# Square Fourier tiles with a tile for the odd column, and rings that begin at one offset

## The chip, the cores and the metric

The kernel runs on one core of a Trainium2 chip, as one program. The metric is the device time of one execution in microseconds (us). The kernel before takes 1317.71 us, the median of three runs from 1316.97 to 1318.9.

## The reference

The input is 256 tokens of 1024 features (float32) and a memory of 256 tokens. Four layers follow, with the mixers Fourier, grouped-query attention, dilated attention, Fourier; each has four heads of attention to the memory beside its mixer, a gate, an output projection, a residual and a layer norm. Two layers of another kind come after them. The change touches the Fourier mixer, which is

```
def fourier_mix(h):
    hg = h.reshape(B, S, 4, D // 4)                 # 4 groups of 256 features
    y = jnp.fft.fftn(hg, axes=(1, 3), norm="ortho").real   # over tokens, and over a group's features
    return y.reshape(B, S, D)

s = jnp.einsum("bshd,bmhd->bhsm", qm, mk) * d**-0.5   # memory attention, 4 heads of 64
o = jnp.einsum("bhsm,bmhd->bshd", softmax(s), mv)
y = (concat([mixer, o]) * silu(gate)) @ w_out         # the branch, 1024 + 256 wide
x = layer_norm(8 ** 0.25 * x + y)
```

and, by the place of some tiles alone, the two layers behind (low-rank attention, a state-space scan, a gated spatial part and a wide MLP).

## The kernel before, in words

**Products.** Every float32 product is made of three TensorE matmuls: each operand is split into a high and a low half (ScalarE copies the high half, VectorE subtracts for the low one), and `Group.add` (L221) issues high by high, high by low, low by high. The 256x1024 activations stand transposed in `xT`, as halves. Weights stream from HBM on SyncE's DMA queue into a ring `raw`; ScalarE (L162) and VectorE (L164) split them into rings `wh` and `wl`.

**Order.** The program is written for a framework that schedules the instructions of each engine from a model of their costs; the order on an engine is that of its schedule, and every engine runs its own in order. Tiles of a ring are given out in turn.

**The rings of operands.** `ph` (20 slots, L399) holds halves of activations in the first four layers, `ph2` (12 slots, L964) in the two layers behind. As the built program places them, the tiles `xT`, `raw`, `wh` and `wl` begin 192 bytes above a multiple of 512. A slot of `ph` takes 2080 bytes, so its slots begin at all sixteen multiples of 32 modulo 512, and those of `ph2` begin at 96. In the products that project to the model's width (512 columns), a tile of `ph` or `ph2` is the stationary operand and `wh` or `wl` the moving one. Such products with `ph2` are 768 in the MLP and 192 in the output projections of the last two layers; those of `ph` are some 480 in the output projections of the first four.

**A Fourier layer** (`layer_fourier`, layers 0 and 3). For each of four groups two PSUM tiles of 258 columns are made, one for each half of the tokens: 129 cosine columns (0 to 128) and 129 sine columns of the transform over features. `split` (L671; ScalarE and VectorE lines L193 and L194) brings each into `uh` and `ul`. The column 128 of the cosines, the odd one, is copied by GpSimd (L673) into `mid`, where it stands in column 32g for group g; the rest of `mid` is zero. `positions(g)` makes the transform over tokens for the 128 regular cosine and sine columns (256-column matmuls into `sc`), adds and subtracts the two parts on VectorE, and moves 127 rows by a DMA on GpSimd's queue (L693) into `sg[0:127, 2g+1]`. `middle()` does the same for the odd columns of all groups: six matmuls into `sc`, a ScalarE copy (L701), and a DMA on GpSimd's queue (L702) that brings four rows into row 127 of `sg`'s blocks 1, 3, 5 and 7. So no block with an odd number is complete before the transfer of L702 has landed.

**What comes behind.** The gates' projections (256-column matmuls `acc<-xT,w`) are turned into `th` by ScalarE (L512; the ring has two tiles), and VectorE combines gate and branch (L513, L515). A combined block c is split by ScalarE and GpSimd (`finish_y`, L545 and L201) and is then the stationary operand of the output projection (`mm_out`), that is `acc<-wh,ph`, `acc<-wl,ph` and `tp<-wh,ph` with 512 columns. L515 makes two blocks at a time, so it always needs a block with an odd number. The memory attention is woven in as `pair_dense`: scores, softmax, transposes of the probabilities (L534, `tp<-ident,pt`), a split into `PTh` and `PTl`, and the products `pv` with the memory's values (`mv_99` and `mv_100` are the high and low halves).

Of the kernel before, what the change touches and what calls it, by code (L numbers as in the profile page):

```python
# [9 lines left out]
F32 = mybir.dt.float32  # L10
# [7 lines left out]
P = 128  # L18
# [58 lines left out]
def kernel(ctx: ExitStack, tc: tile.TileContext, x_in, wall, vec, tabs, small, out, dbg=None):  # L77
    nc = tc.nc
    V, A, G, PE = nc.vector, nc.scalar, nc.gpsimd, nc.tensor
# [11 lines left out]
    def scp(shape):  # L91
        return psum.tile(shape, F32, tag="sc", name="sc", bufs=2)

    def tpp(shape):
        return psum.tile(shape, F32, tag="tp", name="tp", bufs=2)
# [7 lines left out]
    def pt(shape, dt=F32):  # L103
        return ab.tile(shape, dt, tag="P", name="pt", bufs=4)
# [76 lines left out]
    def W(key, i, ahead=AHEAD):  # L181
        n = where[(key, i)]
        while state["split"] <= min(n + ahead, len(order) - 1):
            while state["raw"] <= min(state["split"] + 1, len(order) - 1):
                load_raw(state["raw"])
                state["raw"] += 1
            split_w(state["split"])
            state["split"] += 1
        return wts[n]

    def split(h, l, src, scale=None, eng=None):
        if scale is None:
            A.copy(out=h, in_=src)  # L193
            return (eng or V).tensor_tensor(out=l, in0=src, in1=h.bitcast(F32), op=ALU.subtract).ins  # L194
        else:
            A.activation(out=h, in_=src, func=AF.Copy, scale=scale)
            return (eng or V).scalar_tensor_tensor(
                out=l, in0=src, scalar=scale, in1=h.bitcast(F32), op0=ALU.mult, op1=ALU.subtract).ins
# [49 lines left out]
    def hl(pair, f):  # L248
        return f(pair[0]), f(pair[1])
# [3 lines left out]
    def run(steps):  # L253

        while True:
            try:
                next(steps)
            except StopIteration as e:
                return e.value
# [139 lines left out]
    def ph(shape, dt=F32R):  # L399
        return pool1.tile(shape, dt, tag="ph", name="ph", bufs=20)  # L400
# [48 lines left out]
    for i in range(4):  # L449
# [3 lines left out]
        for c in range(2):  # L453
            for kk in range(2):
                k = 2 * i + kk
# [142 lines left out]
    def tail(key, blk0, by_class=False):  # L598

        half = lambda hf: slice(hf, T, 2) if by_class else slice(hf * P, (hf + 1) * P)  # L600
        ps = yield from proj_N(key, blk0, True, lambda t, k, hf: t[:, k, half(hf)])
        qm = (ph([P, 2, T]), ph([P, 2, T]))
        for hf in range(2):
            t = pool1.tile([P, 512], F32, tag="tq", name="tq", bufs=2)
            th = pool1.tile([P, 256], F32, tag="tqh", name="tqh", bufs=2)
            with tc.high_priority():
                A.activation(out=t[:, 0:256], in_=ps[hf][:, 0:256], func=AF.Copy, scale=0.125)
                A.activation(out=th, in_=ps[hf][:, 256:512], func=AF.Tanh, scale=0.5)
                V.scalar_tensor_tensor(out=t[:, 256:512], in0=th, scalar=1.0, in1=ps[hf][:, 256:512], op0=ALU.add, op1=ALU.mult)
            tp = tpp([P, 4, P])  # L610
            for j in range(4):
                PE.transpose(tp[:, j, :], t[:, j * P:(j + 1) * P], ident)
            split(qm[0][:, :, half(hf)], qm[1][:, :, half(hf)], tp[:, 0:2, :])
            A.copy(out=sg[:, 8:10, half(hf)], in_=tp[:, 2:4, :])
        has_gate.update((8, 9))
        return qm

    def gates(key, blk):
        for b in range(2):
            ps = yield from proj_T(key, blk + b)  # L620
            for j in range(2):
                gate(ps[j], 4 * b + 2 * j)

    def out_and_norm(i, order_, next_order=None):
        gb = []

        def add(hf, blk, ps):
            c = slice(blk * 512, (blk + 1) * 512)
            with tc.high_priority():
                V.scalar_tensor_tensor(out=x[:, hf, c], in0=x[:, hf, c], scalar=ALPHA, in1=ps, op0=ALU.mult, op1=ALU.add)  # L630
                stats(hf, blk)
                if blk == 1:
                    layer_norm(hf, gb, next_order)

        def ready(n):
            if order_[n] not in has_y:
                return False
            if n == 5 and not gb:
                gb.extend(load_gb(i + 1))
                if next_order == "rms":  # L640
                    gn[0] = load_gn(10496)
            for c in order_[n:n + 3]:
                if c in has_y and c not in ys:
                    finish_y(c)
            return True

        ys.clear()
        yield from mm_out(add, f"o{i}", lambda n: (ys[order_[n]][:, 0, :], ys[order_[n]][:, 1, :]), 10, i == 2, ready, i)
        for t in (has_gate, has_branch, has_y):
            t.clear()  # L650
        dump(f"h{i + 1}", x)

    def layer_fourier(i):
        j = i // 3
        key = f"a{j}"
        dc = W(f"dftc{j}", 0)
        dt_ = [W(f"dftt{j}", n) for n in range(2)]
        uv = []

        mid = ph([P, 2, 2, P])  # L660
        G.memset(mid.bitcast(F32), 0.0)
        for g in range(4):
            uh, ul = ph([P, 2, 258]), ph([P, 2, 258])
            for hf in range(2):
                tp = tpp([P, 258])
                gr = Group(tp, 2)
                for kc in range(2):
                    k = 2 * g + kc
                    gr.add((xTh[:, k, hf * P:(hf + 1) * P], xTl[:, k, hf * P:(hf + 1) * P]),
                           hl(dc, lambda t: t[:, kc * 258:(kc + 1) * 258]))  # L670
                split(uh[:, hf, :], ul[:, hf, :], tp)  # L671
            for n, t in enumerate((uh, ul)):
                G.tensor_copy(out=mid[:, n, :, 32 * g:32 * g + 1], in_=t[:, :, 128:129])  # L673
            uv.append((uh, ul))
        qm = run(tail(key, 0))


        odd = [pool1.tile([P, 2, T], F32, tag="odd", name="odd", bufs=2) for _ in range(2)]

        def positions(g):  # L680
            sp = scp([P, 2, T])
            bk = {}
            for part in range(2):
                gr = Group(sp[:, part, :], 2, bk)
                for kc in range(2):
                    gr.add(hl(uv[g], lambda t: t[:, kc, 129 * part:129 * part + P]),
                           hl(dt_[kc], lambda t: t[:, part * T:(part + 1) * T]))
            r = pt([P, T])
            A.copy(out=r, in_=sp[:, 1, :])
            V.tensor_tensor(out=sg[:, 2 * g, :], in0=sp[:, 0, :], in1=r, op=ALU.add)  # L690
            o = odd[g // 2][:, g % 2, :]
            sc_read.append(V.tensor_tensor(out=o, in0=sp[:, 0, :], in1=r, op=ALU.subtract).ins)
            G.dma_start(sg[0:127, 2 * g + 1, :], o[1:128])  # L693

        def middle():
            sp = scp([P, T])
            gr = Group(sp, 2)
            for kc in range(2):
                gr.add(hl((mid[:, 0], mid[:, 1]), lambda t: t[:, kc, :]), hl(dt_[kc], lambda t: t[:, 0:T]))
            r = pt([P, T])  # L700
            sc_read.append(A.copy(out=r, in_=sp).ins)  # L701
            G.dma_start(sg[127:128, 1:8:2, :], r[0:128:32, :])  # L702
            has_branch.update(range(8))

        def fill():
            for g in range(4):
                positions(g)
                yield
            middle()
            yield from gates(key, 1)  # L710
            yield from out_and_norm(i, ORDER[0], "rms" if i == DEPTH - 1 else None)

        weave(fill(), [(lambda: True, lambda m=m: memory_pair(qm, m)) for m in range(2)], 2, 2)
# [145 lines left out]
    def layer_dilated(i):  # L859
# [84 lines left out]
        for hf in range(2):  # L944
            nc.gpsimd.dma_start(x[:, hf, :], scratch[hf * P:(hf + 1) * P, :])

    layer_fourier(0)
    nc.scalar.dma_start(rtab, tabs[:, 0:512].rearrange("p (h k d) -> p h k d", h=2, k=4))
    for hf in range(2):
        t = pt([P, 512])  # L950
# [11 lines left out]
    p2 = ctx.enter_context(tc.tile_pool(name="p2", bufs=1))  # L962

    def ph2(shape, dt=F32R):  # L964
        return p2.tile(shape, dt, tag="ph2", name="ph2", bufs=12)
# [68 lines left out]
    def layer2(l):  # L1034
# [15 lines left out]
        rn = p2.tile([P, 2, 2], F32, tag="rn", name="rn")  # L1050
        kr = p2.tile([P, 2, 1, 32], F32, tag="kr", name="kr")
        dtr = p2.tile([P, 2, 6], F32, tag="dtr", name="dtr")
        cqT = [ph2([P, 2, T]) for _ in range(3)]
        ckvT = [ph2([P, 2, T]) for _ in range(2)]

# [375 lines left out]
        gr = {}  # L1431
# [34 lines left out]
    for hf in range(2):  # L1466
        t = [ph2([P, 512], F32) for _ in range(2)]
# [174 lines left out]
```

## Time and profile before

| what | value |
|---|---|
| median of three runs | 1317.71 us (1316.97 to 1318.9) |
| the profiled execution | 1315.77 us |
| its span | 1314.1 us |
| granted TensorE clock, mean | 0.994 |
| TensorE busy | 1260.3 us, 96% |
| VectorE busy | 979.2 us, 75% |
| ScalarE busy | 751.4 us, 57% |
| GpSimd busy | 187.1 us, 14% |

The span runs from the first to the last instruction; 1.7 us of the execution lie around it. Busy shares are of the span. TensorE's matmuls overlap in their pipeline, so the time from the start of one to the start of the next, its pitch, is what a matmul costs in a dense row, and it is shorter than its printed duration.

### The profile page before, as it was taken

What the parts mean: (1) busy time and instruction counts of PE and PEld (TensorE: products, weight loads), DVE (VectorE), ACT (ScalarE), POOL (GpSimd) and SP (SyncE); (2) the same over time, 40 slices, a digit from 0 to 9 for tenths busy, and PEclk for the clock granted to TensorE, in tenths of its full rate; (3) what the DMA queues carried; (4) which work ended last, traced back from release to release, by engine and by line L of the source; (5) the groups of instructions that cost most, each with busy time, mean ns of one, the idle gap of its engine ahead of it and who ended that gap; (6) DMA issues with size and microseconds to landing.
All of it is one profiled execution on the core that took longest, in us unless ns stands there. A gap on an engine that the chain in (4) does not pass through costs nothing. (4 is left out here: it accounts for less than half of the span.)

```text
span 1314.1 us, 20879 instructions
## 1 busy us (share of the span) xinstructions
PE 1260.3 (96%) x7102; PEld 1063.0 (81%) x7102; DVE 979.2 (75%) x1994; ACT 751.4 (57%) x1689; POOL 187.1 (14%) x290
## 2 busy tenths in 40 slices
PE   7999998899999999998998999999999999999997
PEld 6987796578778778897986897788887897788886
DVE  7788887788777877886777896676666887675654
ACT  5664576655555555663653784565554775565543
POOL 1131500111211211222132201000001201000000
PEclk9999999999999999999998999999999999999999
DMA  8574542354435444455564643476665454476661
GB/s 287 174 216 144 170 153 65 112 177 140 126 120 162 140 148 129 128 176 166 185 194 130 198 137 112 129 243 189 188 186 162 134 153 140 131 223 183 189 191 49
DMA packets 64059, 209.48 MB, mean 159 GB/s; under 512 B 8520, under 2 KB 10192, under 8 KB 63952
## 3 DMA queue, kind: packets, MB, share of 16 engines
q1 hardware_dynamic: 60480, 203.33, 50.6%
q0 software_dynamic: 1888, 3.15, 0.8%
q10 hardware_dynamic: 1584, 1.67, 0.4%
q8 instruction: 56, 0.92, 0.3%
q14 instruction: 51, 0.42, 0.1%
HBM read 204.97 MB, written 2.10 MB: 158 GB/s over the span
## 5 line engine op out<-in xcount | busy, mean ns | idle before, releaser
L164 DVE TENSOR_TENSOR wl<-raw,wh 128x512 fp32r<-128x512 f32 (+3 forms) x756 | 504.8, 695 | 181.0 <-ACT wh L162 167.3
L162 ACT CAST wh<-raw 128x512 fp32r<-128x512 f32 (+3 forms) x756 | 440.9, 607 | 305.4 <-PE acc L221 93.0
L221 PE MATMUL acc<-wh,xT 128*128 128x512 f32 (+3 forms) x1120 | 350.8, 388 | 5.8 <-DVE xT L194 2.5
L221 PEld LDWEIGHTS acc<-wh,xT 128*128 128x128 f32 x1120 | 206.8, 189 | 45.9 <-DVE xT L194 5.1
L221 PE MATMUL acc<-wh,ph 128*128 128x512 f32 (+2 forms) x672 | 225.1, 390 | 6.7 <-ACT ph L545 2.3
L221 PE MATMUL acc<-wl,xT 128*128 128x512 f32 (+3 forms) x560 | 214.6, 384 | 0.2 <-DVE wl L164 0.2
L221 PEld LDWEIGHTS acc<-wh,ph 128*128 128x128 f32 x672 | 125.2, 189 | 38.1 <-ACT ph L193 4.6
L221 PE MATMUL acc<-wl,ph 128*128 128x512 f32 (+2 forms) x336 | 130.4, 388 | 0.0
L221 PE MATMUL acc<-xT,wh 128*128 128x256 f32 x672 | 127.9, 286 | 0.0
L221 PEld LDWEIGHTS acc<-wl,xT 128*128 128x128 f32 x560 | 106.1, 190 | 17.6 <-DVE wl L164 0.5
L221 PEld LDWEIGHTS acc<-xT,wh 128*128 128x128 f32 x672 | 105.9, 191 | 1.4
L221 PE MATMUL sc<-wh,ph 128*128 128x512 f32 (+1 forms) x328 | 104.5, 369 | 0.1
L204 POOL TENSOR_TENSOR rot<-rot,t 128x256 f32<-128x256 f32 (+3 forms) x84 | 61.4, 752 | 253.2 <-DVE t L724 172.2
L221 PE MATMUL acc<-xT,wl 128*128 128x256 f32 x336 | 95.6, 285 | 0.0
L1417 PE MATMUL tp<-xT,wh 128*128 128x512 f32 x224 | 80.9, 395 | 0.0
L221 PEld LDWEIGHTS acc<-wl,ph 128*128 128x128 f32 x336 | 63.8, 190 | 11.5
L221 PEld LDWEIGHTS sc<-wh,ph 128*128 128x128 f32 x328 | 59.8, 188 | 12.2 <-ACT ph L193 0.5
L221 PEld LDWEIGHTS acc<-xT,wl 128*128 128x128 f32 x336 | 64.1, 191 | 0.5
L1418 PE MATMUL tp<-xT,wl 128*128 128x256 f32 x224 | 62.8, 281 | 0.0
L221 PE MATMUL sc<-wl,ph 128*128 128x512 f32 (+1 forms) x164 | 60.9, 371 | 0.0
L365 POOL TENSOR_SCALAR st<-st 128x1 f32<-128x1 f32 x10 | 3.1, 306 | 386.7 <-ACT pt L360 386.7
L201 POOL TENSOR_TENSOR ph<-sg,ph 128x256 fp32r<-128x256 f32 x40 | 36.5, 937 | 128.2 <-ACT ph L545 128.1
(268 smaller groups left out, 2017.6 us busy)
## 6 DMA issues: line engine op xcount, KB each, us to landing
raw<-in_wall_dram SPq DMA_DIRECT2D x338, 512.0 KB, 4.3
raw<-in_wall_dram SPq DMA_DIRECT2D x20, 384.0 KB, 3.6
ph<-in_vec_dram SPq DMA_DIRECT2D x20, 256.0 KB, 5.8
raw<-in_wall_dram SPq DMA_DIRECT2D x8, 422.0 KB, 3.9
gn<-in_vec_dram SPq DMA_DIRECT2D x5, 512.0 KB, 4.8
raw<-in_wall_dram SPq DMA_DIRECT2D x6, 288.0 KB, 3.3
raw<-in_wall_dram SPq DMA_DIRECT2D x6, 256.0 KB, 3.5
x<-in_x_in_dram SPq DMA_DIRECT2D x2, 512.0 KB, 8.2
```

The costliest lines, as they stand in the source:

```text
L162: ih = A.copy(out=h[:, :k], in_=t[:, c]).ins
L164: il = V.tensor_tensor(out=l[:, :k], in0=t[:, c], in1=h[:, :k].bitcast(F32), op=ALU.subtract).ins
L201: G.tensor_tensor(out=out, in0=a, in1=b, op=ALU.subtract)
L204: G.tensor_tensor(out=out, in0=a, in1=b, op=ALU.add)
L221: done[0] = PE.matmul(out=self.out, lhsT=s, rhs=m, start=(i == 1), stop=(i == bk["n"]), skip_group_check=True).ins
L365: G.tensor_scalar(out=v, in0=ssx[hf][:, 0:1], scalar1=ssx[hf][:, 1:2], scalar2=RMS_EPS, op0=ALU.add, op1=ALU.add)
L1417: PE.matmul(out=ps[c], lhsT=h_, rhs=xT[:, k, :, :], start=(k == 0), stop=False, skip_group_check=True)
L1418: done[0] = PE.matmul(out=ps[c][:, 0, :], lhsT=l_, rhs=xTh[:, k, :], start=False, stop=(k == 7), skip_group_check=True).ins
```

## The change

`uh` and `ul` hold two tiles of 128 columns a half, 2048 bytes for each partition and no longer 2064. `split` takes columns 0 to 127 and 129 to 256 of the PSUM tile; column 128 is split from PSUM straight into `mid`, by ScalarE and VectorE (one 128x1 instruction each for every half and group: 8 and 8 a layer), and GpSimd's copies (8 a layer) are gone. The stationary operand in `positions` is indexed accordingly. In the two last layers a tile of 224 bytes that nobody uses stands ahead of the ring `ph2`.

```
         for g in range(4):
-            uh, ul = ph([P, 2, 258]), ph([P, 2, 258])
+            uh, ul = ph([P, 2, 2, P]), ph([P, 2, 2, P])
...
-                split(uh[:, hf, :], ul[:, hf, :], tp)
-            for n, t in enumerate((uh, ul)):
-                G.tensor_copy(out=mid[:, n, :, 32 * g:32 * g + 1], in_=t[:, :, 128:129])
+                split(uh[:, hf], ul[:, hf], tp.rearrange("p (a k) -> p a k", a=2)[:, :, 0:P])
+                split(mid[:, 0, hf, 32 * g:32 * g + 1], mid[:, 1, hf, 32 * g:32 * g + 1], tp[:, 128:129])
...
-                    gr.add(hl(uv[g], lambda t: t[:, kc, 129 * part:129 * part + P]),
+                    gr.add(hl(uv[g], lambda t: t[:, kc, part, :]),
...
         dtr = p2.tile([P, 2, 6], F32, tag="dtr", name="dtr")
+        p2.tile([P, 56], F32, tag="pad", name="pad")
         cqT = [ph2([P, 2, T]) for _ in range(3)]
```

Modulo 512 bytes, the tiles of the built programs begin at:

| tiles | before | after |
|---|---|---|
| `xT`, `raw`, `wh`, `wl` | 192 | 192 |
| `ph`, 20 slots | all multiples of 32 | 320 |
| `ph2`, 12 slots | 96 | 320 |
| `PTh`, `PTl`, `th`, `mkT`, `mv` | 320 | 320 |

The two last layers have the same instructions in the same order on every engine. In the first four the schedule differs at three places: in layer 0, at one small place of layer 2 (the dilated attention), and in layer 3. Two of them follow.

TensorE in layer 0, kernel before, from the last matmuls of `middle` (`sc<-wh,ph` and `sc<-wl,ph`): gates (`acc<-xT`) and transposes (`tp<-ident,pt`) alternate.

```order
L221 MATMUL sc<-wl,ph 128x256
L221 MATMUL sc<-wh,ph 128x256
L221 MATMUL acc<-xT,wl 128x256
L221 MATMUL acc<-xT,wh 128x256 x2
L534 MATMUL tp<-ident,pt 128x128 x2
L221 MATMUL acc<-xT,wl 128x256
L534 MATMUL tp<-ident,pt 128x128 x2
```

This pattern of gates goes on, with the other four transposes in it, and the stretch ends with

```order
L221 MATMUL acc<-xT,wl 128x256
L221 MATMUL pv<-PTh,mv_99 128x512
L221 MATMUL pv<-PTl,mv_99 128x512
L221 MATMUL pv<-PTh,mv_100 128x512
L221 MATMUL pv<-PTh,mv_99 128x512
L221 MATMUL pv<-PTl,mv_99 128x512
L221 MATMUL pv<-PTh,mv_100 128x512
L221 MATMUL acc<-wh,ph 128x512
```

In all 37 gate matmuls stand between `middle` and the first matmul of the output projection (`acc<-wh,ph`). The same place in the changed kernel:

```order
L221 MATMUL sc<-wl,ph 128x256
L221 MATMUL sc<-wh,ph 128x256
L534 MATMUL tp<-ident,pt 128x128 x8
L221 MATMUL pv<-PTh,mv_99 128x512
L221 MATMUL pv<-PTl,mv_99 128x512
L221 MATMUL pv<-PTh,mv_100 128x512
L221 MATMUL pv<-PTh,mv_99 128x512
L221 MATMUL pv<-PTl,mv_99 128x512
L221 MATMUL pv<-PTh,mv_100 128x512
L221 MATMUL acc<-wh,ph 128x512
```

All gates now stand ahead of `middle`'s six matmuls; behind them are 8 transposes and 6 products `pv`.

TensorE in layer 3, changed kernel, from `middle`'s last matmul to the output projection:

```order
L221 MATMUL sc<-wh,ph 128x256
L221 MATMUL acc<-xT,wh 128x256
L221 MATMUL acc<-xT,wl 128x256
L221 MATMUL acc<-xT,wh 128x256 x2
L221 MATMUL acc<-xT,wl 128x256
L221 MATMUL acc<-xT,wh 128x256
L534 MATMUL tp<-ident,pt 128x128 x2
L221 MATMUL acc<-xT,wh 128x256
L534 MATMUL tp<-ident,pt 128x128 x2
L221 MATMUL acc<-xT,wl 128x256
L534 MATMUL tp<-ident,pt 128x128 x4
```

Before, 36 gate matmuls stand in that place, with the transposes among them, and one product `pv` ahead of the output projection's first two; now there are 8 gate matmuls, and four products `pv` follow.

VectorE at the same place of layer 3, before and then after (PTl is the low half of the transposed probabilities, which `pv` needs; `sg` is the branch, whose odd blocks wait for the transfer of L702):

```order
L164 TENSOR_TENSOR wl<-raw,wh 128x512 x4
L515 SCALAR_TENSOR_TENSOR sg<-sg,th 128x512 x2
L194 TENSOR_TENSOR PTl<-tp,PTh 128x512 x2
L513 SCALAR_TENSOR_TENSOR th<-th,acc 128x512
L164 TENSOR_TENSOR wl<-raw,wh 128x512
```

```order
L164 TENSOR_TENSOR wl<-raw,wh 128x512 x4
L515 SCALAR_TENSOR_TENSOR sg<-sg,th 128x512
L194 TENSOR_TENSOR PTl<-tp,PTh 128x512
L515 SCALAR_TENSOR_TENSOR sg<-sg,th 128x512
L194 TENSOR_TENSOR PTl<-tp,PTh 128x512
L513 SCALAR_TENSOR_TENSOR th<-th,acc 128x512 x2
```

One L194 now stands between the two L515; in both kernels the first L515 is ahead of it.

## Rows read from the trace of the kernel before

**Rows 1.** Part 1 of the page: busy time of each engine.

```profile
PE 1260.3 (96%) x7102; PEld 1063.0 (81%) x7102; DVE 979.2 (75%) x1994; ACT 751.4 (57%) x1689; POOL 187.1 (14%) x290
```

**Rows 2.** Windows, layer 0: PE, PEld, DVE, ACT, POOL busy; clock, DMA, GB/s.

```profile
25.00:85.00 60.00, 58.19 (x419) 52.72 (x418) 46.36 (x94) 39.39 (x92) 8.12 (x16) 1.00 0.64 203
```

**Rows 3.** PE timeline, output projection: start, duration, instruction, [idle <-releaser].

```profile
94.16 0.39 PE L221 MATMUL acc<-wh,ph 128*128 128x512 f32 x1
...
96.89 0.40 PE L221 MATMUL acc<-wh,ph 128*128 128x512 f32 x1
...
99.69 0.39 PE L221 MATMUL acc<-wh,ph 128*128 128x512 f32 x1
```

**Rows 4.** Chain that ended last, MLP of the last layer: start, length, step.

```profile
1296.03 5.60 PE acc L221 x24
```

**Rows 5.** ScalarE splits by form: busy and mean ns; idle and releasers.

```profile
L193 ACT CAST ph<-acc 128x128 fp32r<-128x128 f32 x48 | 11.3, 277 | 4.8 <-DVE ph L194 3.4 <-DVE t L724 1.3
```

**Rows 6.** PE timeline, layer 0, from the end of `middle` to the output projection.

```profile
74.75 0.28 PE L221 MATMUL acc<-xT,wl 128*128 128x256 f32 x1
...
76.03 0.40 PE L221 MATMUL acc<-xT,wh 128*128 128x256 f32 x2
...
77.83 0.40 PE L221 MATMUL acc<-xT,wh 128*128 128x256 f32 x2
78.07 0.60 PE L534 MATMUL tp<-ident,pt 128*128 128x128 f32 x4
78.42 0.36 PE L221 MATMUL acc<-xT,wl 128*128 128x256 f32 x1
...
81.99 0.50 PE L221 MATMUL pv<-PTl,mv 128*128 128x512 f32 x1 [0.84 <-DVE PTl L194]
...
82.56 0.39 PE L221 MATMUL acc<-wh,ph 128*128 128x512 f32 x1
```

**Rows 7.** ScalarE timeline, layer 0.

```profile
75.16 0.37 ACT L701 COPY pt<-sc 128x256 f32<-128x256 f32 x1
...
81.50 0.59 ACT L512 ACTIVATE th<-acc 128x512 f32<-128x512 f32 x1
81.99 0.70 ACT L545 CAST ph<-sg 128x256 fp32r<-128x256 f32 x2
```

**Rows 8.** GpSimd timeline, layer 0.

```profile
75.81 0.61 POOL L702 DMA_DIRECT2D sg<-pt  x1 [9.36 <-ACT pt L701]
```

**Rows 9.** VectorE timeline, layer 0.

```profile
80.04 1.30 DVE L515 SCALAR_TENSOR_TENSOR sg<-sg,th 128x512 f32<-128x512 f32 x2
```

**Rows 10.** Line L702: its transfers, one in layer 0, one in layer 3.

```profile
DMA to landing us min/median/max: 3.0/3.6/4.1
```

**Rows 11.** Line L693: its eight transfers.

```profile
DMA to landing us min/median/max: 2.1/2.5/3.9
```

**Rows 12.** PE timeline, layer 3, the same place.

```profile
663.53 0.40 PE L221 MATMUL acc<-xT,wh 128*128 128x256 f32 x2
...
669.40 0.51 PE L221 MATMUL acc<-wh,ph 128*128 128x512 f32 x1 [0.29 <-ACT ph L545]
```

**Rows 13.** GpSimd timeline, layer 3.

```profile
664.61 0.61 POOL L702 DMA_DIRECT2D sg<-pt  x1 [9.15 <-ACT pt L701]
```

**Rows 14.** VectorE timeline, layer 3.

```profile
667.67 1.30 DVE L515 SCALAR_TENSOR_TENSOR sg<-sg,th 128x512 f32<-128x512 f32 x2 [0.55 <-DMA sg<-pt]
668.88 1.28 DVE L194 TENSOR_TENSOR PTl<-tp,PTh 128x512 fp32r<-128x512 f32 x2
```

**Rows 15.** PE timeline, layer 2, scores and transposes of the dilated attention.

```profile
378.92 0.66 PE L534 MATMUL tp<-ident,pt 128*128 128x128 f32 x4
...
383.00 0.44 PE L534 MATMUL tp<-ident,pt 128*128 128x128 f32 x2 [0.69 <-DVE pt L836]
```

**Rows 16.** Windows, columns as in rows 2: three stretches with long waits of TensorE.

```profile
612.00:622.00 10.00, 6.90 (x32) 5.78 (x32) 8.29 (x15) 1.93 (x4) 4.83 (x8) 0.83 0.57 175
698.00:712.00 14.00, 8.35 (x31) 6.56 (x29) 8.48 (x15) 4.96 (x13) 3.42 (x6) 0.76 0.08 28
786.00:797.00 11.00, 9.04 (x40) 6.46 (x41) 8.50 (x23) 4.96 (x15) 2.92 (x3) 0.84 0.36 135
```

## The prediction

> **What bounds the kernel now.** I read the page's busy times first. TensorE works through 1260.3 of 1314.1 us, VectorE through 75%, ScalarE through 57%, GpSimd through 14% [rows 1]. So only two things move the time: the pitch of the matmuls, and the some 54 us in which TensorE has nothing. The windows say where the change lies in that picture. Around the first Fourier layer TensorE is busy for 58.19 of 60.00 us at full granted clock, with VectorE at 46.36 and ScalarE at 39.39 [rows 2]: dense, with room on the other engines. There, work that is put earlier or later costs nothing; a hole costs its whole length. The timelines around `middle` come next, since its transfer is the one long delay that the reordering touches, then the pitch of the products on `ph` and `ph2`, then the stretches with a lowered clock.
>
> **The odd column and the small splits.** GpSimd loses 16 copies; ScalarE and VectorE gain 16 instructions of 128x1 each. The nearest row for one is a split of 128x128 at 277 ns [rows 5]. All 32 on the path would be 32 x 0.277 = 8.9 us; nothing hidden anywhere gives 0. I exclude a gain: no one needs `mid` before `middle`, some tens of us later. They lie beside dense TensorE work; in these 60 us ScalarE has 20.6 and VectorE 13.6 us free [rows 2], and a layer's eight take 2.2 us on each. I take 0. What could fail is that the two PSUM tiles are held longer by two small instructions; if each of the 16 tiles held TensorE for one of them, that is 4.4 us, which I keep as the outer edge.
>
> **The pitch.** Where the first output projection reads a tile that begins at 192 modulo 512 (as `wh` does), 12 matmuls start from 94.16 to 96.89: 227.5 ns each. The next tile begins at 320, and its 12 run from 96.89 to 99.69: 233.3 ns [rows 3]. In the last MLP with `ph2` at 96, 24 matmuls take 5.60 us: 233.3 ns [rows 4]. So an offset has a price of some 6 ns, but 320 is no better than 96 by these rows. The change puts 960 stationary operands of `ph2` from 96 to 320: 0 by the row at 320, and 960 x 5.8 ns = 5.6 us less if they fell to the pitch at 192. One tile is thin evidence and any surprise points down, so I take -1.0, near the row at 320, and keep both ends. The `ph` tiles of the first layers lose one slot in 16 that stood at 192: some 480 products / 16 x 5.8 ns = 0.2 us more, inside that choice.
>
> By the Trainium skill (TensorE: Matmul & The Clock Gate, section Back-to-back issue gap) an isolated matmul's gap depends on its columns and the clock alone, about 216 ns at 512 columns. The rows disagree, with 227 and 233 ns for the same columns. By that rule this term would be 0 and the sum 1.0 us higher.
>
> **Layer 0: `middle` comes after the gates.** Before, 7.81 us lie from the end of `middle` (74.75) to the output projection (82.56) [rows 6]. In them are 37 gate matmuls at 0.120 (15 from 76.03 to 77.83 take 1.80), 8 transposes at 0.0875 (four from 78.07 to 78.42), and 6 `pv` at 0.233: 4.44 + 0.70 + 1.40 = 6.54 us. So 1.27 us are empty, mostly at the product that VectorE's PTl releases at 81.99 [rows 6].
>
> What runs beside this work is a chain that does not care what TensorE does. The copy of L701 starts at 75.16 [rows 7], GpSimd issues the transfer at 75.81 [rows 8], it lands 4.1 us later (the longer of L702's two) [rows 10], and L515 starts at 80.04 [rows 9]. L515 takes 0.69 (a row of two takes 1.30, and in rows 14 two starts lie 1.21 / 2 = 0.61 apart), ScalarE's L512 0.59 and the first L545 0.40 (two in 0.70) [rows 7], and 0.17 passes from there to the matmul (81.99 + 0.40 to 82.56): 80.04 + 0.69 + 0.59 + 0.40 + 0.17 = 81.89, which is 7.1 us behind `middle`. L512 stands ahead of L545 on ScalarE in the new order too, and waits for L515 to release one of the two `th` tiles.
>
> After, only 8 transposes and 6 `pv` are left to do in these 7.1 us: 2.1 us. The gates have gone ahead of `middle`, into dense time, and pull nothing forward there. Idle becomes 7.1 - 2.1 = 5.0 instead of 1.27: **+3.7 us**. Queued behind the waiting L515 on VectorE are the weights' splits and the third gate; TensorE's next products all need the first block. If the transfer landed in 2.1, the shortest of its neighbour L693 [rows 11], it would be +1.7; I take 4.1 since it is this transfer's own.
>
> **Layer 3.** The same place: `middle` ends at 663.53, the projection starts at 669.40 [rows 12], 5.87 us for 36 gates, 8 transposes and one `pv`: 4.32 + 0.70 + 0.23 = 5.25, empty 0.6. The transfer is issued at 664.61 [rows 13] and L515 starts at 667.67, released by it [rows 14], 4.14 us behind `middle`; it landed in 3.0 [rows 10]. Now the order on VectorE matters as well: the first PTl stands behind the first L515, and four `pv` stand ahead of the projection. So 4.14 + 0.60 (to L515's end as its successor sees it) + 0.69 (PTl, again two in 1.28) = 5.43, then three `pv` that need it, 0.70, and the projection starts 6.1 us behind `middle`. Left to do are 8 gates, 8 transposes and 4 `pv`: 0.96 + 0.70 + 0.93 = 2.6. Idle 3.5 for 0.6: **+2.9 us**, between 2.0 (landing 2.1) and 4.0 (landing 4.1).
>
> By the Trainium skill (SBUF — State Buffer, section The DMA setup-cost knee) a small transfer pays a roughly fixed cost of about 2 us. The two here took 3.0 and 4.1 us, so the rows are above it. With 2.0 in both, the two terms would be about +1.6 and +1.9.
>
> **Layer 2.** The softmax between scores and the last transposes took 4.1 us (378.92 to 383.00) [rows 15]. In the new order 19 matmuls of 512 columns, 4.3 us, stand over it: 0.1 for what doesn't fit, 0 to 0.9 if the last step of the softmax is exposed as it is now, with 0.69 idle.
>
> **Sum.** 3.7 + 2.9 + 0.1 - 1.0 + 0 = +5.7 us. Against the profiled execution that is 1315.8 + 5.7 = 1321.5. That execution lies 1.9 us under the median of the runs, and I forecast a median: 1317.7 + 5.7 = **1323.4 us**.
>
> **Rivals.**
>
> *The clock falls in the new holes.* The granted clock was 0.83 in a stretch of 10 us, 0.76 in one of 14 and 0.84 in one of 11 [rows 16]: TensorE fell to the lower level of its two (1.2 GHz against 2.4) behind holes. The last cost 11 x 0.16 = 1.8 us of work. It speaks for this that the new holes, 5.0 and 3.5 us, are long; against it that they are broken by transposes and `pv`. One fall gives 1325.2, two 1327.0.
>
> *The transfers land sooner.* Nothing of their queue changes, but L693's landed in 2.1 at best and the gates' weights now pass the DMA engines earlier. Then 1.7 + 2.0 + 0.1 - 1.0 = +2.8: 1320.5 us.
>
> *The pitch falls after all (not slower).* If a common offset in a ring is what counts, and not the one offset of 192, all 960 products of `ph2` run at 227.5: 3.7 + 2.9 + 0.1 - 5.6 = +1.1, 1318.8 us. Against it speaks the tile at 320 [rows 3]; for it, that this tile stood among others at other offsets. If the output projections of the first four layers follow, 480 x 5.8 ns = 2.8 more: 1316.0. With the shorter transfers as well it would be 2.0 + 0.9 = 2.9 us less again, 1313.1, faster than before. The point from which this side wins is a pitch of 226 ns or less over all of `ph2`: 960 x 7 ns = 6.7 us, as much as the holes cost.
>
> *The holes don't come.* The order is fixed in the program, so they can only be filled by another wait that vanishes; the 1.27 and 0.6 us that are empty now are already set off. I give this no chance of its own.
>
> **How the numbers follow.** A run of this kernel can be told from no change at about 0.2%, 2.6 us: under 1315.1 is faster, over 1320.3 slower. The forecast has 0.50 (by itself 1321 to 1325); a fall of the clock on top 0.15; shorter transfers 0.12, half of it over the bound; the lower pitch 0.16, within 0.2%; lower pitch and shorter transfers together 0.07, faster. Slower is 0.50 + 0.15 + 0.06 = 0.71, same 0.06 + 0.16 = 0.22, faster 0.07. The range leaves out the last case and part of the next to last below, and two falls of the clock above: 1317.5 to 1326.5.
>
> **What would show it.** In the changed kernel's profile: in layer 0, after `middle`'s six matmuls, transposes and `pv` as one short block, and then an idle of some 2 us or more before the first output projection, released by ScalarE's L545, about 7 us behind `middle`; in layer 3 a `pv` on PTl that waits 2.5 to 3 us for VectorE's L194, itself behind an L515 that the transfer releases. The chain's steps of 24 matmuls in the last MLP stay at 5.5 to 5.6 us; 5.46 would be the rival. The span outside these places is the same to 1 us, the last two layers above all. I am wrong if TensorE is idle for under 2 us at either place, if the MLP's steps are at 5.46, or if the lost time lies where the small splits are, before `middle`.

## The result and the profile after

The changed kernel takes 1325.19 us, the median of six runs (1322.72 to 1327.25), against 1316.78 us for six runs of the kernel before (1313.71 to 1318.9): a ratio of 1.0068 with a 95% interval of 1.0057 to 1.0079, so some 8 to 9 us more. The forecast was 1323.4 us, 5.7 more. The profiled execution took 1324.08 us, its span is 1322.3, 8.2 longer than before.

Part 1 of the page of the changed kernel, which answers to [rows 1]:

```profile
PE 1266.1 (96%) x7102; PEld 1069.0 (81%) x7102; DVE 979.5 (74%) x2010; ACT 752.6 (57%) x1705; POOL 180.0 (14%) x274
```

The number of matmuls is the same, and TensorE is busy 5.8 us longer: the same work takes longer, which is a first hint at the clock. The rest is 2.4 us more of nothing to do.

Where the time goes is read by looking for one instruction that ends each layer in both traces: the first transposes of the new `x` (L308) after layers 0, 2 and 3. TensorE timeline of the kernel before, then of the changed kernel:

```profile
116.97 1.29 PE L308 MATMUL sc<-ident,x 128*128 128x128 f32 x8 [0.67 <-DVE x L430]
...
616.24 1.94 PE L308 MATMUL sc<-ident,x 128*128 128x128 f32 x8 [3.10 <-DVE x L430]
...
702.36 1.97 PE L308 MATMUL sc<-ident,pt 128*128 128x128 f32 x8 [3.67 <-DVE pt L374]
```

```profile
120.47 0.63 PE L308 MATMUL sc<-ident,x 128*128 128x128 f32 x4 [0.67 <-DVE x L430]
...
621.58 0.66 PE L308 MATMUL sc<-ident,x 128*128 128x128 f32 x2 [3.08 <-DVE x L430]
...
710.24 1.97 PE L308 MATMUL sc<-ident,pt 128*128 128x128 f32 x8 [3.66 <-DVE pt L374]
```

The delay is 3.5 us after layer 0, 5.3 after layer 2, 7.9 after layer 3 and 8.2 at the end. So it arises in the two Fourier layers and once between them, and the last two layers add 0.3.

**Layer 0.** TensorE timeline of the changed kernel, the place of [rows 6]:

```profile
77.96 1.17 PE L534 MATMUL tp<-ident,pt 128*128 128x128 f32 x8
80.14 0.49 PE L221 MATMUL pv<-PTh,mv 128*128 128x512 f32 x1 [1.01 <-ACT PTh L193]
81.10 0.50 PE L221 MATMUL pv<-PTl,mv 128*128 128x512 f32 x1 [0.46 <-DVE PTl L194]
...
84.55 0.80 PE L221 MATMUL acc<-wh,ph 128*128 128x512 f32 x1 [1.34 <-ACT ph L545]
85.14 0.63 PE L221 MATMUL acc<-wl,ph 128*128 128x512 f32 x1
...
88.50 0.39 PE L221 MATMUL tp<-wl,ph 128*128 128x512 f32 x1
```

`middle` ends at 77.96, where the transposes start, and the output projection starts at 84.55: 6.6 us with 2.1 us of work, so 4.5 us empty at full clock for 1.27 before. The waits stand where the prediction put them, the last one ended by L545. The chain beside it, GpSimd and then VectorE:

```profile
79.37 0.61 POOL L702 DMA_DIRECT2D sg<-pt  x1 [8.78 <-ACT pt L701]
```

```profile
82.88 1.29 DVE L515 SCALAR_TENSOR_TENSOR sg<-sg,th 128x512 f32<-128x512 f32 x2 [1.24 <-DMA sg<-pt]
```

VectorE now waits 1.24 us for the transfer; before, no such wait stood at its L515 [rows 9]. The two transfers of L702 landed in 2.8 and 3.4 us (3.0 and 4.1 before [rows 10]).

**Layer 3**, TensorE and then VectorE, the places of [rows 12] and [rows 14]:

```profile
672.06 0.28 PE L221 MATMUL acc<-xT,wh 128*128 128x256 f32 x1
...
674.92 0.49 PE L221 MATMUL pv<-PTh,mv 128*128 128x512 f32 x1 [0.87 <-ACT PTh L193]
677.25 0.51 PE L221 MATMUL pv<-PTl,mv 128*128 128x512 f32 x1 [1.84 <-DVE PTl L194]
677.59 0.64 PE L221 MATMUL pv<-PTh,mv 128*128 128x512 f32 x2
678.06 0.40 PE L221 MATMUL acc<-wh,ph 128*128 128x512 f32 x1
```

```profile
675.90 0.69 DVE L515 SCALAR_TENSOR_TENSOR sg<-sg,th 128x512 f32<-128x512 f32 x1 [0.59 <-DMA sg<-pt]
676.51 0.68 DVE L194 TENSOR_TENSOR PTl<-tp,PTh 128x512 fp32r<-128x512 f32 x1
```

The first PTl is ready in time but stands behind an L515 that the transfer holds, and TensorE waits 1.84 us for it. From `middle` (672.06) to the projection (678.06) are 6.0 us with 2.6 of work.

**The clock.** The granted clock is the share of its full clock that TensorE was given. Windows of the changed kernel (columns as in rows 2), around layer 0's hole and in layer 2:

```profile
80.00:90.00 10.00, 8.06 (x22) 5.71 (x23) 7.85 (x12) 6.47 (x17) 5.42 (x7) 0.66 0.60 193
384.00:394.00 10.00, 8.74 (x53) 6.91 (x52) 8.92 (x26) 5.69 (x17) 1.20 (x4) 0.83 0.01 2
```

In the kernel before both stretches have a granted clock of 1.00. TensorE works at the lower of its two levels for 6.8 us from 81 us on: the matmuls from 85.14 to 88.50 start 0.42 us apart (eight in 3.36), where a full clock has 0.233. In layer 2 it does so for 3.4 us, in a piece that has no new hole, whose instructions and waits are the same before (the reordered place of layer 2 lies behind it): the 18 small score matmuls of L238, before and after,

```profile
384.42 1.29 PE L238 MATMUL sc<-ph 64*128 64x128 f32 x18
```

```profile
388.12 1.71 PE L238 MATMUL sc<-ph 64*128 64x128 f32 x18
```

3.4 us at half the rate are 1.7 of the 1.8 us that come between the end of layer 0 and that of layer 2. So the clock took 1.7 us there and about 1.5 behind layer 0's hole (the eight matmuls above), some 3.2 of the 8.2 us of this execution. In layer 3's hole it did not fall here (granted clock 1.00 from 674 to 684 us).

Over all runs the mean granted clock is 0.9895 for the changed kernel (six runs) and 0.9927 for the one before (23 runs, with a mean time of 1315.9). Multiplying each run's time by its clock takes the lost rate out, as if all of it had been work: 1311.3 us against 1306.3, so 4.3 of the 9.3 us between the means would go with the clock. That is an estimate from above, since a low clock costs nothing where TensorE waits: for the two profiled executions the same sum would leave only 1.6 us (1307.8 against 1306.2), less than the waits that stand in the trace.

### The profile page after: what moved, and what is told of

It reads as the page before. It is cut to its first block, busy times and chain, and to the rows that moved or that the text cites. A ratio compares the mean times of both kernels' runs of the same rounds, so it can differ in the third digit from the quotient of the medians.

```text
span 1322.3 us, 20883 instructions
## 1 busy us (share of the span) xinstructions
PE 1266.1 (96%) x7102; PEld 1069.0 (81%) x7102; DVE 979.5 (74%) x2010; ACT 752.6 (57%) x1705; POOL 180.0 (14%) x274
## 5 line engine op out<-in xcount | busy, mean ns | idle before, releaser
L194 DVE TENSOR_TENSOR PTl<-tp,PTh 128x512 fp32r<-128x512 f32 x76 | 48.5, 663 | 4.9 <-ACT PTh L193 4.5
```

## The experiments

The theory is that the order causes the loss: with no gates left behind `middle`, its transfer is uncovered, and the clock falls in the holes. The rivals are the places of the tiles and the small splits. Each kernel was timed beside the kernel before.

**One part each.** The odd column alone, with the old tiles:

```
-            for n, t in enumerate((uh, ul)):
-                G.tensor_copy(out=mid[:, n, :, 32 * g:32 * g + 1], in_=t[:, :, 128:129])
+                split(mid[:, 0, hf, 32 * g:32 * g + 1], mid[:, 1, hf, 32 * g:32 * g + 1], tp[:, 128:129])
```

> The kernel before with one part of the change: the odd column is split straight from PSUM into its tile, the tiles keep 258 columns and their places. TensorE's order is then that of the changed kernel, row for row. Theory (the order is the cause: the transfer behind `middle` has no gates left to hide it, and the clock falls in the holes): +6 to +9 us against the kernel before, with the waits before the first output projection in layers 0 and 3 as in the changed kernel. Rival (the new places of the tiles cost the time): 0 to +2 us.

Measured: 1324.29 us, ratio 1.0066 (1.0053 to 1.0078). Its holes, in TensorE's timeline:

```profile
84.80 0.50 PE L221 MATMUL acc<-wh,ph 128*128 128x512 f32 x1 [1.83 <-ACT ph L545]
...
675.72 0.50 PE L221 MATMUL pv<-PTl,mv 128*128 128x512 f32 x1 [2.15 <-DVE PTl L194]
```

So this part alone gives the whole loss. Its trace also parts the holes from the clock, since here the clock stayed up behind layer 0's hole and fell in layer 3's:

```profile
80.00:90.00 10.00, 7.12 (x28) 5.26 (x29) 8.33 (x13) 6.77 (x18) 5.61 (x8) 1.00 0.62 195
674.00:684.00 10.00, 8.28 (x29) 6.64 (x30) 7.48 (x12) 4.90 (x13) 5.65 (x7) 0.83 0.65 201
```

```profile
118.86 1.29 PE L308 MATMUL sc<-ident,x 128*128 128x128 f32 x8 [0.66 <-DVE x L430]
...
619.72 1.94 PE L308 MATMUL sc<-ident,x 128*128 128x128 f32 x8 [3.07 <-DVE x L430]
...
710.23 1.41 PE L308 MATMUL sc<-ident,pt 128*128 128x128 f32 x8 [3.65 <-DVE pt L374]
```

Layer 0 costs 1.9 us here for 3.5 in the changed kernel, and layer 3 4.4 for 2.5: a fall of the clock at a hole is worth 1.6 to 1.9 us, and which hole has one differs between the two traces. The other part is the 224 bytes ahead of `ph2`:

```
+        p2.tile([P, 56], F32, tag="pad", name="pad")
```

> The kernel before with the other part: the 224 bytes ahead of the ring of the last two layers, so that its slots begin at 320 and no longer at 96 modulo 512. The order of every engine is that of the kernel before. Theory: 0, within 1 us, and 24 matmuls of the last MLP in 5.6 us as before. Rival (a common offset lowers the pitch): -5.6 us, steps of 5.46 us. Rival (tiles behind the ring, now 32 above a multiple of 64, read slower): +1 to +3 us.

Measured: 1317.02 us, ratio 1.0008 (0.9999 to 1.0016); 24 matmuls of the last MLP took 5.57 us against 5.60 [rows 4]. The common offset of 320 gives nothing.

**Put the cover back.** Six pieces of the gates, 36 matmuls, are tied behind `middle` (`hold` is its last matmul):

```
+                    with (tc.issue_after(hold) if hold is not None and 4 * i + c >= 16 - 6 else ExitStack()):
                         gr[c].add(...)
...
             middle()
-            yield from gates(key, 1)
+            yield from gates(key, 1, done[0])
```

> The changed kernel with 36 gate matmuls of a Fourier layer tied behind `middle`, so that 5.25 us of TensorE work lie between it and the output projection in both layers; the small splits and all places stay. Theory: the holes shrink to some 0.6 to 1.5 us, no fall of the clock there, and the time is that of the kernel before within 2 us, some 8 us under the changed kernel. Rival (places or small splits cost the time): it stays at +6 to +9 us.

Measured: 1320.87 us, ratio 1.0048 (1.0034 to 1.0062): only some 3 us of the loss came back, for the 8 that I expected, though the waits ahead of both projections shrank to 0.78 us. TensorE's timeline in layer 0 shows why:

```profile
75.14 0.36 PE L221 MATMUL sc<-wh,ph 128*128 128x256 f32 x1 [1.46 <-ACT pt L575]
...
82.88 0.50 PE L221 MATMUL acc<-wh,ph 128*128 128x512 f32 x1 [0.78 <-ACT ph L546]
```

`middle` writes into one of two `sc` tiles, which the second pair's softmax (the exponential, ScalarE) has to free first. The gates that now stand behind `middle` had filled that wait; it is 1.46 us long, and 0.55 in layer 3. The amount of filling work in the layer is limited, and the two waits share it. By the L308 transposes layer 0 costs 1.2 us in this execution and layer 3 3.2; at the start of layer 3, which the edit does not touch, the granted clock is 0.76 from 613 to 627 us, for 0.88 at the same place of the kernel before (612 to 626), and that is 1.7 us of it.

**`middle` earlier.**

```
             for g in range(4):
+                if g == 2:
+                    middle()
                 positions(g)
                 yield
-            middle()
```

> The changed kernel with one edit in the order of the program: `middle` is called ahead of the third `positions`, and no longer behind the fourth. 13.3 us (layer 0) and 15.4 us (layer 3) of TensorE work then lie between `middle` and the output projection, and 8.9 and 10.7 us behind the last `positions`, more than the some 7 us of the chain from a copy over the transfer to the first block. Theory (uncovered transfer): the waits on ScalarE's L545 and on PTl are gone or under 0.5 us, no fall of the clock there, and the time is 8 to 11 us under the changed kernel, so 0 to -2 us against the kernel before. Rival (places or small splits cost a part): it stays 3 us or more above the kernel before.

Measured: 1321.34 us, ratio 1.0040 (1.0026 to 1.0053). My expectation was wrong. The waits behind `middle` are gone, but others of like size stand later, inside the output projections of layers 0 and 3:

```profile
97.49 0.51 PE L221 MATMUL acc<-wh,ph 128*128 128x512 f32 x1 [2.48 <-ACT ph L545]
...
687.89 0.50 PE L221 MATMUL acc<-wh,ph 128*128 128x512 f32 x1 [1.39 <-ACT ph L545]
```

The second memory pair has been pushed behind the gates, and its block is the last that the projection needs. So this edit too only moved the wait.

**The transfer on another queue.**

```
-            G.dma_start(sg[127:128, 1:8:2, :], r[0:128:32, :])
+            nc.scalar.dma_start(sg[127:128, 1:8:2, :], r[0:128:32, :])
```

> The changed kernel with the transfer of `middle` issued on ScalarE's queue in place of GpSimd's. The order of TensorE in layer 0 is that of the changed kernel. Theory (the landing of this transfer sets the end of the holes): the issue comes some 0.6 us earlier and the landing takes 2 to 3 us for 2.8 to 3.4, so the output projection starts 1 to 2 us earlier in each of the two layers, -2 to -4 us against the changed kernel, +4 to +7 us against the kernel before. Rival (the wait is set by the memory attention's softmax and splits): no difference from the changed kernel.

Measured: 1323.98 us, ratio 1.0067 (1.0053 to 1.0082), no difference from the changed kernel. The chain did get shorter, but by little. VectorE and TensorE in layer 0:

```profile
82.33 1.29 DVE L515 SCALAR_TENSOR_TENSOR sg<-sg,th 128x512 f32<-128x512 f32 x2 [0.78 <-DMA sg<-pt]
```

```profile
84.00 0.72 PE L221 MATMUL acc<-wh,ph 128*128 128x512 f32 x1 [1.56 <-ACT ph L545]
```

`middle` ended at 77.87, so the projection starts 6.1 us behind it for 6.6; in layer 3 it is 5.7 for 6.0. In layer 3 the order is not quite the same: both L515 stand ahead of PTl again, and three `pv` behind the projection's first matmuls. In layer 0 the issue came only 0.3 us earlier (79.08 for 79.37). L515 starts 3.25 us behind it there and 3.21 in layer 3, for 3.51 and 2.79 on GpSimd's queue: on the whole the landing is no shorter. That the transfer releases L515 is in the rows of both; that it could be had cheaper was a wrong guess.

**Fill the holes.** In the changed kernel 25 matmuls of zeros stand in the waits (the result is unused):

```
+        if warm:
+            with tc.issue_after(turned[0]):
+                last = keep_warm(warm[0])
...
+        warm = (4, 2, 7) if i == 0 else (4, 8, 0)
```

> The changed kernel with 25 matmuls of zeros, whose result nobody reads, put by the order into the waits behind `middle`: 4, 2 and 7 in layer 0 (behind the transposes, behind the first `pv`, ahead of the output projection), 4 and 8 in layer 3. They are shorter than the waits, so they delay nothing, and TensorE is kept at work. Theory (a part of the loss is the clock that falls in the holes, the rest the holes themselves): no half clock at 81 to 88 us and at 675 to 680 us, the granted clock goes from 0.9895 to 0.991 to 0.993, and the time falls by 2 to 4 us against the changed kernel, to +5 to +6 us against the kernel before; the first output projections start at the same distance from `middle`. Rival (the lower clock in these runs has nothing to do with the holes): no difference from the changed kernel, +8 to +9 us.

Measured: 1321.56 us, ratio 1.0040 (1.0026 to 1.0054), granted clock 0.9930. TensorE in layer 0, and the windows where the clock had fallen:

```profile
82.39 1.68 PE L391 MATMUL sc<-zero 128*128 128x512 bf16 x7
84.32 0.50 PE L221 MATMUL acc<-wh,ph 128*128 128x512 f32 x1 [0.25 <-ACT ph L546]
84.66 0.39 PE L221 MATMUL acc<-wl,ph 128*128 128x512 f32 x1
```

```profile
80.00:90.00 10.00, 9.59 (x40) 6.37 (x40) 7.90 (x12) 6.84 (x18) 5.64 (x8) 1.00 0.62 203
384.00:394.00 10.00, 8.74 (x59) 6.95 (x57) 9.01 (x26) 6.40 (x18) 2.66 (x6) 1.00 0.01 2
```

The projection starts 6.3 us behind `middle` (6.6 in the changed kernel), and the matmuls that follow run at full clock. More matmuls, and less time. The L308 transposes place the gain:

```profile
118.48 1.29 PE L308 MATMUL sc<-ident,x 128*128 128x128 f32 x8 [0.68 <-DVE x L431]
...
618.46 1.29 PE L308 MATMUL sc<-ident,x 128*128 128x128 f32 x8 [3.07 <-DVE x L431]
...
707.01 1.94 PE L308 MATMUL sc<-ident,pt 128*128 128x128 f32 x8 [3.75 <-DVE pt L374]
```

Layer 0 costs 1.5 us for 3.5; all but 0.3 of these 2.0, by which the chain is shorter, go with the clock. Layer 3, where the clock had not fallen in the changed kernel's trace, costs 2.4 for 2.5. What stays, +4.9 us, is in the main the holes of the two layers. In layer 2 the clock stayed up too, at the same waits as before, with nothing filled there and some other instructions of the layer in another order, so the rest of the gain, some 1.1 us up to the end of layer 2, is not the filling's. In three traces the clock fell at this place (the changed kernel, the odd column alone, the other queue), in the nine others it did not; no run here says what decides it.

**The offset.** `ph2` at the offset of the weights (96 bytes ahead of it), the order kept:

```
+        p2.tile([P, 24], F32, tag="pad", name="pad")
```

> The kernel before with 96 bytes ahead of the ring of the last two layers, so that its slots begin at 192 modulo 512, where the weights' tiles begin too. Same order. Theory (a stationary operand at the offset of the moving one has a pitch of 227.5 ns and no longer 233.3): 960 x 5.8 ns = -5.6 us, steps of 5.46 us for 24 matmuls in the last MLP. Rival (the offset does nothing; the one tile at 192 was faster for another reason): 0, steps of 5.60 us.

Measured: 1312.21 us, ratio 0.9970 (0.9961 to 0.9979). Its chain, the place of [rows 4]:

```profile
1290.47 5.44 PE acc L221 x24
```

That is 226.7 ns a matmul. The whole gain is 3.9 us (2.8 to 5.1 by the interval), less than the 5.6 expected. Is 192 a good place, or is it the agreement with the weights? `wh` and `wl` at 320 with `ph2` at 320, `xT` left at 192:

```
         load_raw(n)
+    wp.tile([P, 32], F32, tag="wpad", name="wpad")
...
+        p2.tile([P, 24], F32, tag="pad", name="pad")
```

> The kernel before, same order, with the rings `wh` and `wl` moved by 128 bytes to begin at 320 modulo 512, and `ph2` at 320 too; `xT` stays at 192. Theory of a match (the stationary operand at the moving operand's offset is what lowers the pitch): the products on `ph2` at 227 to 228 ns, those on `xT` at 232 to 233: 960 x 5 ns less and some 1200 to 1700 x 4.5 ns more, +1 to +4 us in all. Rival (192 is the good offset of the stationary operand, whatever the other has): products on `xT` stay at 227 to 229 ns and those on `ph2` at 232 to 233: 0. Third (192 is good for the moving operand): all at 232 to 233 ns, +5 to +8 us.

Measured: 1315.40 us, ratio 0.9995 (0.9984 to 1.0005). The chain in the last MLP, and 21 products on `xT` in layer 2, here and then in the kernel before:

```profile
1294.40 5.44 PE acc L221 x24
```

```profile
371.93 0.39 PE L221 MATMUL acc<-wl,xT 128*128 128x512 f32 x1
...
376.81 0.39 PE L221 MATMUL acc<-wl,xT 128*128 128x512 f32 x1
```

```profile
371.93 0.39 PE L221 MATMUL acc<-wl,xT 128*128 128x512 f32 x1
...
376.70 0.39 PE L221 MATMUL acc<-wl,xT 128*128 128x512 f32 x1
```

`ph2` is as fast at 320 as it was at 192, and the products on `xT`, whose place did not change, became slower: 4.88 / 21 = 232.4 ns for 4.77 / 21 = 227.1. So it is the agreement of the two operands, and no place by itself. Gain and loss cancel in the time, which by itself would fit the rival's 0 better than the theory's +1 to +4; the rows decide. By the Trainium skill (TensorE: Matmul & The Clock Gate, section Back-to-back issue gap) the gap of an isolated matmul depends on its columns and the clock alone; these rows, of dense streams with the same columns, have 226.7 and 232.4 ns.

**Together.** First with the square tiles and `middle` earlier, both rings at 192:

```
+    pool1.tile([P, 96], F32, name="pad1")
...
+        p2.tile([P, 24], F32, tag="pad", name="pad")
```

> `middle` called earlier as in the run before, the square tiles of the change, and both rings `ph` and `ph2` moved to begin at 192 modulo 512 (384 bytes ahead of `ph`, 96 ahead of `ph2`). Theory: the pitch of all some 1440 products on these rings falls from 232 to 233 ns to 227 to 228 ns: some -4 us for `ph2`, as the ring at 192 showed, and 480 x 4.5 ns = -2 us for `ph`, beside the missing holes: -6 to -9 us against the kernel before. Rival (the holes come back in another place): -4 us or less of gain.

Measured: 1316.10 us, ratio 0.9999 (0.9988 to 1.0010). Of the 6 to 9 us expected nothing came: the pitch gives back what the moved waits cost, and no more. Then with the kernel before's order kept row for row; `ph` gets slots of a multiple of 512 bytes:

```
     def ph(shape, dt=F32R):
-        return pool1.tile(shape, dt, tag="ph", name="ph", bufs=20)
+        t = pool1.tile([P, 640], dt, tag="ph", name="ph", bufs=16)
+        return ...          # the first columns of t, in the shape asked for
```

> The kernel before, its order kept row for row on every engine, with both operand rings at 192 modulo 512, the offset of the weights: `ph` has 16 slots of 2560 bytes in place of 20 of 2080 (tiles keep their 258 columns, and begin 384 bytes later), and 96 bytes stand ahead of `ph2`. Theory (what counts is that the stationary operand has the offset of the moving one): -4 us from `ph2`, as measured alone, and 480 products of `ph` at 227.5 to 229 for 232.3 ns, -2 us: -6 us against the kernel before. Rival (with the smaller ring the schedule's order waits for slots): -4 us or less.

Measured: 1311.91 us, ratio 0.9963 (0.9950 to 0.9975). The mean pitch of 498 products of `ph` in the trace went from 232.3 to 229.4 ns, that is 1.4 us. By the medians it gains 4.8 us, for 6 expected. This kernel is faster than both; over `ph2` alone at 192 its gain lies inside the intervals.

## Why the prediction was right

**The sign and the mechanism held.** The holes stand where the steps put them, are ended by what they named (L545 in layer 0; PTl behind L515 in layer 3), and their chains took 6.6 and 6.0 us for 7.1 and 6.1 forecast. The single waits are shorter than its signs said, 1.34 us at L545 for "some 2 us or more" and 1.84 at PTl for 2.5 to 3, because each hole falls into pieces: 1.01, 0.46 and 1.34 in layer 0, 0.87 and 1.84 in layer 3, 2.8 and 2.7 in all. Its sign of being wrong, TensorE idle for under 2 us at either place, is met by these last waits taken alone, and not by the sums.

**Term by term**, from the delays at the ends of the layers:

| term | forecast | profiled execution |
|---|---|---|
| layer 0 | +3.7 | +3.5 |
| layer 2 | +0.1 | +1.8 |
| layer 3 | +2.9 | +2.5 |
| pitch, and all that comes behind | -1.0 | +0.3 |
| sum | +5.7 | +8.2 |

Layer 0's agreement is in part luck. The holes cost 4.5 - 1.27 = 3.2 us, and the clock about 1.5 more (eight matmuls of the projection, 3.36 us for 1.87). Some 1.2 us were won ahead of `middle`, which the prediction did not see: 37 gate matmuls more than before had run by then, 37 x 0.120 = 4.4 us of work, and `middle` ended only 3.2 us later. Where they were won stays open: a wait of 0.83 us at 22.16 has become 0.20, but in the run with the other queue it is 0.82, and `middle` ends as early.

**Two terms were off.** The step "I take -1.0" for the pitch should have stayed with the row at 320 that it quoted: the padding alone took 0.03 us from 24 matmuls, and nothing measurable from the time. The rival of a common offset is refuted, and the place at 192 was a real price of 5 to 6 ns, but one of agreement. The step that left the clock to a rival with 0.15 was the larger fault: the clock fell behind layer 0's hole and in layer 2, and took some 3 us of the 8. A fall at the holes belonged in the sum, since all three stretches with long waits in [rows 16] had it; the one in layer 2 stands at no new hole, and the prediction names nothing there. With both corrected the sum would have been about +6.7 from the holes and two falls at 1.7, +10: nearer, and on the other side of what was measured. That the median fell on the 1325.2 of "one fall" is luck: two falls counted, and the 1.2 us ahead of `middle` set part of them off. The number is also flattered by its base: six runs of the kernel before have a median 0.9 us under the three that it started from, so 1.8 us off in the time are 2.7 off in the difference.

**The small splits and the shorter transfers.** The splits cost nothing that shows: TensorE came to the end of `middle` earlier for its work, not later. They come with the new order in every run that has them, so no run prices them in the old one. Landings of 2.8 and 3.4 us lay between the bounds of 2.1 and 4.1, in their middle, so the rival of 2.1 did not come.

## What to carry to other kernels

A split that costs nothing by its length can still cost by the order that a scheduler builds around it: read what work is left behind a transfer, before and after, and count the hole as its chain less that work. Putting cover back at one place takes it from another, so look for the next wait before you call a hole filled; and price a hole on TensorE with the clock that can fall behind it: at the holes here it took 1.6 to 1.9 us, in some traces and not in others. For float32 matmuls with 512 moving columns, it is worth laying stationary and moving tiles at the same offset modulo 512 bytes: here 3.9 us for 960 of them.

## What the runs showed of the hardware that I had not expected

A matmul of 128x512 has a pitch of 227 ns where its stationary operand begins at the offset of the moving one modulo 512 bytes, and mostly of 231 to 234 where it does not: so at 192 and 192 and at 320 and 320, and moving the weights alone slowed the products of a tile that stayed. One group does not fit: the products `pv` of the memory attention have both operands at 320 and took 231 to 232 ns; they are few (25 in the trace of before), and why was not tried.
